# Down projection of groups 0 and 1 as seven products per pair of output halves, in a stage of its own behind the walks, with operands passed through device memory

## The chip, the cores and the metric

The kernel runs on one core of a Trainium2 chip. The metric is the device time of one execution in microseconds (us). Engines are named as the profile names them: PE is TensorE (PEld its weight loads), DVE is VectorE, ACT is ScalarE, POOL is GpSimd, SP is the engine in whose queue most DMAs are issued. L126 is line 126 of the kernel.

## The reference, cut to what matters

One decoder layer on 1024 prompt tokens and 8 x 4 decode tokens, 1056 in all, of width 1024, in float32: a mixing sub-layer (pooling and windowed attention), a dense feed-forward of width 2816, and a per-layer input gated by a sigmoid.

```
x = x + _rms(mix, n_mix_post)
f = _rms(x, n_ffn_pre)
f = (jax.nn.silu(f @ w_gate) * (f @ w_up)) @ w_down
x = x + _rms(f, n_ffn_post)
x = x + jax.nn.sigmoid(x @ w_ple_gate) * (p @ w_ple)
```

The change is about `@ w_down`: a (1056 x 2816) by (2816 x 1024) product.

## The kernel before

**Tokens and numbers.** Tokens stand in columns, in three groups of 352 (`G`, `N`); features stand in partitions, 128 at a time. Each float32 product is made of three matmuls: every operand is split into a rounded high part and the rest (`split`, L163: ACT casts, DVE subtracts), and `gemm` (L291) issues high x high, high x low, low x high. All matmuls come from `mm` (L124), so all have line L126; all splits have L164 (ACT) and L165 (DVE), and are told apart by their tiles.

**Walks.** The hidden width is 22 chunks of 128, two to a slab, 11 slabs. `WALK` visits slabs 0 to 4 for group 2 alone, slabs 5 to 10 for all three groups, then slabs 0 to 4 again for groups 0 and 1. `gate_up` (L984) makes one chunk (a slot). For group 2 it makes gate and up directly, 24 matmuls each. For groups 0 and 1 it uses seven products instead of eight (a scheme of Winograd's): the 2 x 2 blocks are (group 0, group 1) x (gate, up) x two halves of the inner dimension; products P1, P2 (on B21), P4 (on T4), S2, S3, S1, S4, 12 matmuls each, 84 in a slot. Their operands B11, B21, B22, T1 to T4 (`f7`) are made once before the walks. The weights of S1 to S4 are sums and differences of the gate and up weights, formed in place in the raw tiles by four POOL operations (`w_sums`, L958) after the raw tiles have been split as they are; then the sums are split too (`sh`, `sl`).

**Down, before.** After the first products of the next slab, `downs` (L1134) multiplies the slab's hidden tile: per group eight output chunks (m) of 6 matmuls, 48 per group and slab, each evicted from PSUM into the sum `o` (ACT copies the first slab's, DVE adds the others, L1065). So a slot that follows a finished slab holds 48 more matmuls for each group walked. The hidden values stay in SBUF (`hid_put`, L955), split into `hid`.

**Weights.** `ITEMS` lists all weight work in the order of use; `need` (L270) makes each item a few ahead (`LOOK` = 4). Raw tiles (`wr`) have three buffers (`W_RAW`), loaded by SP in order; split tiles (`wp`) have eight, that is four pairs. A slot of `gate_up` takes a raw tile for gate and one for up, and four pairs: gate, up, and two of sums.

**Order.** PE's instructions in this part are kept in program order; the other engines' queues are ordered by a scheduler when the program is built, and each engine runs its queue in that order. `turn` and `chain` (L852, L865) spread the steps of a generator (`ffn_steps`, `ple_steps`) over the matmuls issued: `share` sets how densely, and the second argument of `chain` after how many matmuls it begins.

**The end, before.** Behind the walks: one `ple_out` of group 2, the last down products of group 0 and then of group 1, 48 matmuls each; `ple_steps(0)` starts 24 matmuls after group 0's last, `ple_steps(1)` 54 after group 1's. `ple_steps` scales by the norm and the gain and adds the residual (L1104, L1108), makes the operands of a further seven-product scheme for the per-layer gate (`e_sum`, L1082: T1 to T4), while PE runs seven more `ple_out` of group 2, 30 matmuls each, then four `ple_first` (L1188), then four `ple_rest` (L1201).

## Time and profile before

| | before |
|---|---|
| time, median of 3 runs | 1134.59 us (1134.0 to 1137.2) |
| span of the profiled execution | 1132.5 us |
| PE busy | 1111.7 us, 7067 matmuls |
| PEld busy | 1087.4 us |
| DVE busy | 783.6 us |
| ACT busy | 454.3 us |
| POOL busy | 199.0 us |
| DMA | 102.16 MB, mean 90 GB/s |
| granted PE clock, mean | 0.995 |

The span runs from the first to the last instruction of one profiled execution; the times of the runs are of other executions, and their median lies 2.1 us above that span. Busy time is the time in which an engine had an instruction under way; matmuls overlap one another, so the pace of PE is read from how many start in a stretch. Idle time before an instruction is put down to what released it (`<-`).

### The profile page before, as it was taken

To read this page: it belongs to the slowest core of one execution; us is meant where nothing else is said; L and a number is where in the kernel's file an instruction comes from. 1 tells how busy PE (TensorE), PEld (TensorE's weight loads), DVE (VectorE), ACT (ScalarE), POOL (GpSimd) and SP (SyncE) were. 2 spreads that over 40 slices of the span, in tenths; PEclk is the share of its full clock that TensorE was granted. 3 is DMA by queue.
4 is the path that set the end of the run, shared out by engine and by line. 5 is a ranking of instruction groups with operands and counts; after the bars stand their busy time and mean duration, and the time that the engine had idled before them with its cause. 6 is when DMAs were issued, how large, how long until landed. Compare 5 with 4: busy or idle time off the path is not lost. (4 is left out here: it accounts for less than half of the span.)

```text
span 1132.5 us, 17606 instructions
## 1 busy us (share of the span) xinstructions
PE 1111.7 (98%) x7067; PEld 1087.4 (96%) x7067; DVE 783.6 (69%) x1283; ACT 454.3 (40%) x793; POOL 199.0 (18%) x165
## 2 busy tenths in 40 slices
PE   8999999999999999999999999999999999999797
PEld 8999987799999999999999999999999999999697
DVE  6666457876888965355554556547887877789786
ACT  7322266764555523331321313123424334364432
POOL 0044032200000042011111101111141132100231
PEclk9999999999999999999999999999999999999899
DMA  8121310172553312111110212122112222427041
GB/s 285 56 69 56 113 50 20 44 274 74 187 189 117 131 38 76 38 53 60 38 57 19 75 38 75 38 88 76 61 52 94 75 69 94 143 82 258 31 156 58
DMA packets 35985, 102.16 MB, mean 90 GB/s; under 512 B 4260, under 2 KB 14788, under 8 KB 35904
## 3 DMA queue, kind: packets, MB, share of 16 engines
q1 hardware_dynamic: 34576, 99.27, 25.8%
q10 hardware_dynamic: 1328, 1.77, 0.5%
q8 instruction: 55, 0.90, 0.3%
q14 instruction: 26, 0.21, 0.1%
HBM read 90.92 MB, written 10.11 MB: 89 GB/s over the span
## 5 line engine op out<-in xcount | busy, mean ns | idle before, releaser
L126 PE MATMUL b<-hid,wh 128*128 128x352 f32 x1056 | 252.7, 322 | 1.4 <-DVE o L1104 0.8
L164 ACT CAST wh<-wr 128x1024 fp32r<-128x1024 f32 (+1 forms) x135 | 138.4, 1029 | 249.3 <-PE b L126 205.6
L126 PE MATMUL b<-fh,wh 128*128 128x352 f32 x712 | 230.5, 324 | 0.0
L126 PE MATMUL b<-fl,wh 128*128 128x352 f32 x712 | 228.8, 321 | 0.0
L126 PE MATMUL b<-fh,wl 128*128 128x352 f32 x712 | 228.7, 321 | 0.0
L968 POOL TENSOR_TENSOR wr<-wr 128x512 f32<-128x512 f32 x52 | 74.3, 1428 | 738.7 <-DVE wl L165 451.9
L165 DVE TENSOR_TENSOR wl<-wr,wh 128x1024 fp32r<-128x1024 f32 (+1 forms) x135 | 165.4, 1229 | 40.2 <-ACT wh L164 39.9
L126 PEld LDWEIGHTS b<-hid,wh 128*128 128x128 f32 x1056 | 182.5, 188 | 2.2 <-PE b L126 1.1
L126 PE MATMUL b<-hid,wl 128*128 128x352 f32 x528 | 169.1, 320 | 0.0
L1065 DVE TENSOR_TENSOR o<-o,b 128x352 f32<-128x352 f32 x240 | 115.0, 514 | 29.5 <-PE b L126 29.4
L126 PEld LDWEIGHTS b<-fl,wh 128*128 128x128 f32 x712 | 134.4, 189 | 0.0
L126 PE MATMUL b<-fh,sh 128*128 128x352 f32 x416 | 134.3, 323 | 0.0
L126 PEld LDWEIGHTS b<-fh,wh 128*128 128x128 f32 x712 | 134.2, 188 | 0.0
L126 PEld LDWEIGHTS b<-fh,wl 128*128 128x128 f32 x712 | 134.1, 188 | 0.0
L126 PE MATMUL b<-fh,sl 128*128 128x352 f32 x416 | 133.5, 321 | 0.0
L126 PE MATMUL b<-fl,sh 128*128 128x352 f32 x416 | 133.3, 320 | 0.0
L165 DVE TENSOR_TENSOR sl<-wr,sh 128x1024 fp32r<-128x1024 f32 x52 | 63.5, 1222 | 84.5 <-ACT sh L164 84.5
L164 ACT CAST sh<-wr 128x1024 fp32r<-128x1024 f32 x52 | 53.9, 1047 | 144.4 <-POOL wr L968 104.8
L126 PE MATMUL b<-h,wh 128*128 128x352 f32 x480 | 105.8, 326 | 1.5 <-ACT h L379 1.1
L126 PEld LDWEIGHTS b<-hid,wl 128*128 128x128 f32 x528 | 98.9, 187 | 0.0
L126 PEld LDWEIGHTS b<-h,wh 128*128 128x128 f32 x480 | 82.5, 190 | 2.4 <-ACT h L379 1.3
L126 PEld LDWEIGHTS b<-fl,sh 128*128 128x128 f32 x416 | 78.3, 188 | 0.0
(175 smaller groups left out, 1695.4 us busy)
## 6 DMA issues: line engine op xcount, KB each, us to landing
wr<-in_w_gu_dram SPq DMA_DIRECT2D x64, 512.0 KB, 3.3
wr<-in_w_dn_dram SPq DMA_DIRECT2D x32, 512.0 KB, 3.3
wr<-in_w_pg_dram SPq DMA_DIRECT2D x18, 512.0 KB, 3.5
x<-in_x_dram SPq DMA_DIRECT2D x6, 704.0 KB, 10.6
x1d<-x SPq DMA_DIRECT2D x6, 704.0 KB, 3.6
x<-x1d SPq DMA_DIRECT2D x6, 704.0 KB, 5.5
out_y_dram<-yo SPq DMA_DIRECT2D x24, 176.0 KB, 1.9
wr<-in_w_out_b_dram SPq DMA_DIRECT2D x8, 512.0 KB, 4.2
```

Of the source, the lines that this page charges most:

```text
L126: ins = te.matmul(*args, **kw)
L164: fix(se.copy(hi, src))
L165: fix(ve.tensor_tensor(lo, src, hi.bitcast(F32), op=ALU.subtract))
L968: ge.tensor_tensor(out, a, b, op=op)
L1065: ve.tensor_tensor(o, o, v, op=ALU.add)
```

## The change

The down product of group 2 stays where it was. For groups 0 and 1 it leaves the walks and becomes a stage behind them, `down7`, as seven products per pair of output halves instead of eight: the 2 x 2 blocks are now (group 0, group 1) x (even, odd chunk of a slab) x (output columns 0 to 511, 512 to 1023).

- **Operands.** `gate_up` ends in `pair_put`. After a slab's first slot it stages B11 and, after a POOL subtraction, T1; after the second B21, B22 and, after three POOL subtractions, T2, T3 and T4. `stage` splits each (ACT and DVE: seven splits per slab, four before) and, when both slabs of a set are there, writes the tile to device memory (`xd`; 35 DMAs of 704 KB and 7 of half that). The slabs are grouped in the order of the walk into five sets of two and one of a single slab (slab 4). Four new buffers (`hk`) hold the values meanwhile; `tmp` has five buffers instead of six, and the pool of activation tiles 29 instead of 27.
- **Weights.** `q_load` loads the quarters of `w_down` of a set (`wq`, 512 KB). The quarters of P1, P2 and P4 are split as they are; after P4's split, `q_sum` forms the sums of S1, S3, S2, S4 in place on POOL, which are then split.
- **The stage.** `STEPS` has 19 steps: all seven products on sets 0 and 1, five (P1, P2, P4, S2, S3) on sets 2 and 3, the same five on sets 4 and 5, then S1 and S4 on sets 2 to 5. A step makes four output chunks; with two sets of two slabs that is 48 matmuls. `x_get` loads the operands (`xo`) of the current step and the next two. The first seven steps copy PSUM into seven sums `u` (ACT), the later ones add (DVE); on the last use the sums are combined (`finished` also takes the squares for the norm and applies the gain, on ACT, for all groups).
- **The end.** `ple_steps(0)` starts 24 matmuls into the last two steps (S1, S4), `ple_steps(1)` 24 after them; then come all eight `ple_out` of group 2, then `ple_first` and `ple_rest` as before. `ple_steps` no longer applies the gain: per half a multiplication by the norm and one addition.

**VectorE in the late walks.** These are DVE's rows from the multiplication that ends one chunk for groups 0 and 1 (`u`) to the first evictions of the next (`p`). `sl` and `wl` are the low parts of split weights, `hid` the low part of a hidden value, `c` and `p` evictions of products, `fl` is an operand of the per-layer gate. Before, from a slab's first chunk to its second:

```order
L165 TENSOR_TENSOR sl_8211<-wr_8029,sh_8210 128x1024
L1046 TENSOR_TENSOR u_8251<-u_8251,p_8031 128x352
L165 TENSOR_TENSOR hid_8217<-u_8251,hid_8217 128x352
L1002 TENSOR_TENSOR c_8325<-p_8310,b_8326 128x352
L165 TENSOR_TENSOR fl_8340<-x_7811,fh_8339 128x1408
L165 TENSOR_TENSOR wl_8232<-wr_8136,wh_8231 128x1024
L165 TENSOR_TENSOR wl_8305<-wr_8214,wh_8304 128x1024
L1002 TENSOR_TENSOR p_8310<-p_8310,b_8368 128x352
```

And now, from a slab's second chunk to the next slab, where `st` is a staged operand; `c_7779`, `c_7919` and `u_7764` are POOL's results for T2, T4 and T3:

```order
L168 TENSOR_TENSOR sl_7868<-wr_7731,sh_7867 128x1024
L1136 TENSOR_TENSOR u_7904<-u_7904,p_7826 128x352
L168 TENSOR_TENSOR st_7956<-u_7904,st_7956 128x352
L168 TENSOR_TENSOR st_7960<-c_7779,st_7960 128x352
L1094 TENSOR_TENSOR c_7992<-p_7977,b_7993 128x352
L168 TENSOR_TENSOR wl_7887<-wr_7824,wh_7886 128x1024
L168 TENSOR_TENSOR st_7964<-c_7919,st_7964 128x352
L168 TENSOR_TENSOR st_7968<-u_7764,st_7968 128x352
L168 TENSOR_TENSOR wl_7972<-wr_7871,wh_7971 128x1024
L1094 TENSOR_TENSOR p_7977<-p_7977,b_8041 128x352
```

Instead of one `hid` there are four staged splits, and the second `wl` (`wr_7871`, the up weights of the slot after the one that begins here) stands behind all of them.

**SP at the end of the walks.** These are SP's rows there. Before, only weights and a residual (`x1d`) are loaded:

```order
L174 DMA wr_9289<-in_w_gu_dram 128x1024
L174 DMA wr_9394<-in_w_ple_dram 128x1024
L174 DMA wr_9472<-in_w_pg_dram 128x1024
L174 DMA wr_9493<-in_w_dn_dram 128x1024
L1099 DMA x_9867<-x1d_2466 128x1408
```

Now come the last spills (`xd`) of slab 4 and then the first operands (`xo`):

```order
L1024 DMA xd_8554<-st_8551 128x704
L1024 DMA xd_8559<-st_8556 128x704
L1024 DMA xd_8565<-st_8562 128x704
L1024 DMA xd_8571<-st_8568 128x704
L1024 DMA xd_8577<-st_8574 128x704
L1185 DMA xo_8579<-xd_4842 128x1408
L1185 DMA xo_8581<-xd_5797 128x1408
L1185 DMA xo_8583<-xd_5029 128x1408
L1185 DMA xo_8585<-xd_5984 128x1408
L1185 DMA xo_8587<-xd_5043 128x1408
L1185 DMA xo_8589<-xd_5998 128x1408
```

The loads of `xo`, which read what was written long before (`xd_4842`, `xd_5797`), stand behind the writes of the last slab.

The core of the diff:

```diff
-A_SLOTS = 27
+A_SLOTS = 29
...
-        return spool.tile([P, n], dt, tag="tmp", bufs=6, name=nm(s), padded_shape=[P, NX])
+        return spool.tile([P, n], dt, tag="tmp", bufs=5, name=nm(s), padded_shape=[P, NX])
+
+    def kept(s):
+        return spool.tile([P, N], F32, tag="hk", bufs=4, name=nm(s))
...
+    ORDER = list(range(AHEAD, NSLAB)) + list(range(AHEAD))
+    SETS = [ORDER[i : i + 2] for i in range(0, NSLAB, 2)]
+    QUARTER = {"P1": "11", "P2": "12", "P4": "22"}
+    FIVE, TWO = ("P1", "P2", "P4", "S2", "S3"), ("S1", "S4")
+    OPERAND = {"P1": "B11", "P2": "B21", "P4": "T4", "S2": "T2", "S3": "T3", "S1": "T1", "S4": "B22"}
+    STEPS = [(k, (0, 1)) for k in FIVE + TWO]
+    STEPS += [(k, at) for at in ((2, 3), (4, 5)) for k in FIVE]
+    STEPS += [(k, (2, 3, 4, 5)) for k in TWO]
+    WDN = {}
+    for k, at in STEPS:
+        for e in at:
+            WDN[k, e] = item("quarter" if k in QUARTER else "dsum", k, e)
...
+    def q_load(q, e):
+        if (q, e) not in quarters:
+            n = len(SETS[e])
+            t = act_tile([P, n, 512], s="wq")
+            s0 = SETS[e][0]
+            row, col = int(q[1]) - 1, int(q[0]) - 1
+            nc.sync.dma_start(t, w_dn[s0 : s0 + n, col, :, row, :].rearrange("s p n -> p s n"))
+            quarters[q, e] = t
+        return quarters[q, e]
...
+    def q_sum(k, e):
+        out, a, b, op = {
+            "S1": ("22", "21", "22", ALU.add),
+            "S3": ("21", "11", "21", ALU.subtract),
+            "S2": ("11", "22", "11", ALU.subtract),
+            "S4": ("12", "12", "11", ALU.subtract),
+        }[k]
+        ge.tensor_tensor(q_load(out, e), q_load(a, e), q_load(b, e), op=op)
...
+            elif kind == "quarter":
+                made[i] = q_split(q_load(QUARTER[js[0]], js[1]))
+                if js[0] == "P4":
+                    for n in ("S1", "S3", "S2", "S4"):
+                        q_sum(n, js[1])
...
-    def hid_put(g, slot, ht):
-        split(new_hid[g][:, slot, :], new_hid[g][:, SLAB + slot, :], ht)
+    def hid_put(slot, ht):
+        split(new_hid[0][:, slot, :], new_hid[0][:, SLAB + slot, :], ht)
+
+    def stage(key, pair, src):
+        e = next(i for i, ps in enumerate(SETS) if pair in ps)
+        i = SETS[e].index(pair)
+        if (key, e) not in staged:
+            staged[key, e] = act_tile([P, 2, 2, N], F32R, "st")
+        t = staged[key, e]
+        split(t[:, i, 0, :], t[:, i, 1, :], src)
+        if i == len(SETS[e]) - 1:
+            d = dpool.tile([P, 2, 2, N], F32, name=nm("xd"))
+            nc.sync.dma_start(d[:, : i + 1], t[:, : i + 1].bitcast(F32))
+            spilled[key, e] = d
+
+    def pair_put(pair, slot, h0, h1):
+        def sub(out, a, b):
+            ge.tensor_tensor(out, a, b, op=ALU.subtract)
+        if slot == 0:
+            stage("B11", pair, h0)
+            sub(h0, h1, h0)
+            stage("T1", pair, h0)
+            evens[:] = h0, h1
+            return
+        t1, b12 = evens
+        stage("B21", pair, h0)
+        stage("B22", pair, h1)
+        sub(t1, h1, t1)
+        stage("T2", pair, t1)
+        sub(h0, h0, t1)
+        stage("T4", pair, h0)
+        sub(b12, h1, b12)
+        stage("T3", pair, b12)
...
-        hid_put(1, slot, u3)
+        pair_put(pair, slot, c21, u3)
...
+    def x_get(n):
+        if n < len(STEPS):
+            k, at = STEPS[n]
+            for e in at:
+                key = OPERAND[k]
+                if (key, e) not in xops:
+                    w = len(SETS[e])
+                    t = act_tile([P, 2, 2, N], F32R, "xo")
+                    nc.sync.dma_start(t[:, :w].bitcast(F32), spilled[key, e][:, :w])
+                    xops[key, e] = t
+
+    def down7(n):
+        k, at = STEPS[n]
+        final = n >= len(STEPS) - len(FIVE + TWO)
+        for i in range(n, n + 3):
+            x_get(i)
...
+        def part(j, e):
+            wh, wl = need(WDN[k, e], 2)
+            x = xops[OPERAND[k], e]
+            cols = slice(j * P, (j + 1) * P)
+            ops = [(wh[:, i, cols], wl[:, i, cols], x[:, i, 0, :], x[:, i, 1, :]) for i in range(len(SETS[e]))]
+            gemm(banks[j][:, :N], ops, e == at[0], e == at[-1])
+            turn(3 * len(ops))
...
+            if n < len(FIVE + TWO):
+                se.copy(u[k], v)
+                continue
+            add(u[k], u[k], v)
...
-    hid[:] = new_hid
-    for m in range(FIRST):
+    chain(ple_steps(0), 24)
+    down7(len(STEPS) - 2)
+    down7(len(STEPS) - 1)
+    share[0] = 0.7
+    chain(ple_steps(1), 24)
+    for m in range(KC):
         ple_out(m, 2)
-    for m in range(KC):
-        last_down(END, m, 0)
-    chain(ple_steps(0), 24)
-    for m in range(KC):
-        last_down(END, m, 1)
-    chain(ple_steps(1), 54)
-    for m in range(FIRST, KC):
-        ple_out(m, 2)
-    finish(chains[:1])
+    finish(chains[:-1])
```

More of the change, by code (lines that the diff above doesn't have):

```diff
@@ L286, in need @@
             for kind, js in ITEMS[i + 1 : i + 3]:
-                for j in js:
-                    w_load(j)
+                if kind not in ("quarter", "dsum"):
+                    for j in js:
+                        w_load(j)
+            for kind, js in ITEMS[i + 1 : i + 7]:
+                if kind in ("quarter", "dsum"):
+                    q_loads(kind, js)
         return made[k]
@@ L982, in quarter, with gate_up @@
         return tuple(t[:, 4 * h : 4 * h + 4, :] for t in w)
-    def gate_up(items, slot, gs, pending):
+    def gate_up(items, pair, slot, gs, pending):
         ig, iu, is_ = items
@@ L1019, in gate_up @@
             ve.tensor_tensor(sl, sl, direct(wu), op=ALU.mult)
-        for g in gs:
+        if 2 in gs:
             if slot == 0:
-                new_hid[g] = half(g, F32R, "hid")
-        if 2 in gs:
-            hid_put(2, slot, sl)
+                new_hid[0] = half(2, F32R, "hid")
+            hid_put(slot, sl)
         if pending and 0 not in gs:
@@ L1039, in gate_up @@
         ve.tensor_tensor(c21, c21, c11, op=ALU.mult)
-        hid_put(0, slot, c21)
         p5 = product(s["S1"], f7["T1"])
@@ L1130, in ple_steps @@
                 yield 20, 0
-    END = len(WALK) - 1
     def downs(n):
-        s, gs = WALK[n]
         hid[:] = old_hid
-        for half_m in (range(4), range(4, KC)):
-            for g in (2, 0, 1):
-                for m in half_m:
-                    if g in gs:
-                        (last_down if g == 2 and s == NSLAB - 1 else down)(n, m, g)
-        if s == NSLAB - 1:
+        for m in range(KC):
+            down(n, m)
+            if WALK[n][0] == NSLAB - 1:
+                finished(m, 2)
+        if WALK[n][0] == NSLAB - 1:
             share[0] = 0.1
@@ L1150, in trunk_kernel @@
         for i in range(SLAB):
-            gate_up(WGU[n][i], i, gs, (lambda: downs(n - 1)) if i == 0 and n else None)
+            first = i == 0 and n and 2 in WALK[n - 1][1]
+            gate_up(WGU[n][i], s, i, gs, (lambda: downs(n - 1)) if first else None)
+    share[0] = 0.3
+    for n in range(len(STEPS) - 2):
+        down7(n)
     finish(list(chains))
-    share[0] = 0.7
     def ple_end(gate, wp, m, g):
```

116 lines of the change are left out of this document (80 added, 36 removed).

## The prediction

> **What bounds it now.** I read the page's busy table, then the stretches, then who waits for whom, then the order of time in one of the late slots. The columns of a stretch are each engine's busy time, its instructions in brackets, granted clock, DMA share, GB/s.
>
> ```profile
> PE 1111.7 (98%) x7067; PEld 1087.4 (96%) x7067; DVE 783.6 (69%) x1283; ACT 454.3 (40%) x793; POOL 199.0 (18%) x165
> 500.00:600.00 100.00, 100.00 (x632) 100.00 (x631) 56.94 (x96) 24.37 (x36) 15.96 (x12) 1.00 0.16 53
> 900.00:1000.00 100.00, 100.00 (x632) 100.00 (x631) 77.03 (x125) 39.95 (x57) 22.13 (x16) 1.00 0.32 110
> PE b L126 <- ACT p L1196: 5.9, 1, 5.9
> PE b L126 <- DVE dg L325: 1.2, 2, 0.8
> SPq L174 <- DVE sl L165: 470.8, 48, 28.6
> ```
>
> TensorE is the bound: 632 matmuls in 100 us, 0.158 us each at full clock, and the longest wait of PE in the run is one of 5.9 us in the tail. So each matmul taken away is worth 0.158 us, as long as everything else still keeps ahead. The last row shows what may not: weight loads sit in SP's queue until VectorE has finished a split (`sl`) that frees one of three raw buffers. That costs PE nothing today.
>
> **Matmuls removed.** All three groups' down products read `hid`:
>
> ```profile
> L126 PE MATMUL b<-hid,wh 128*128 128x352 f32 x1056 | 252.7, 322 | 1.4 <-DVE o L1104 0.8 <-DVE hid L165 0.6
> L126 PE MATMUL b<-hid,wl 128*128 128x352 f32 x528 | 169.1, 320 | 0.0
> L1065 DVE TENSOR_TENSOR o<-o,b 128x352 f32<-128x352 f32 x240 | 115.0, 514 | 29.5 <-PE b L126 29.4
> L1108 DVE SCALAR_TENSOR_TENSOR x<-o,c,x 128x352 f32<-128x352 f32 x24 | 15.2, 661 | 0.0
> ```
>
> 1584 for three groups, 1056 for groups 0 and 1. Seven products take 7 x 11 pairs x 4 x 3 = 924. 132 fewer at 0.158: **-20.9 us**. Of VectorE's 240 adds of 0.51 us into `o`, 160 go and 76 into the seven sums come; ScalarE evicts the first round (28 copies for 16) and takes over the scaling from the 24 operations of 0.66. VectorE, at 69%, becomes freer by this, and PE does not wait for any of it at present (its wait list has only single waits of about a microsecond besides the one above): nothing.
>
> **The tail.** PE's columns around its one long wait:
>
> ```profile
> 1060.00:1065.00 5.00, 1.48 (x10) 1.19 (x8) 5.00 (x4) 0.73 (x1) 0.00 (x0) 1.00 0.00 0
> 1065.00:1070.00 5.00, 2.65 (x9) 2.65 (x10) 3.72 (x4) 2.43 (x4) 3.56 (x2) 0.58 0.00 0
> 1070.00:1075.00 5.00, 5.00 (x26) 5.00 (x25) 0.90 (x1) 1.99 (x3) 2.82 (x3) 0.74 0.00 0
> ```
>
> 45 matmuls run where 95 fit: 50 x 0.158 = 7.9 us lost, 5.9 of it idle and 2.0 at the clock that is granted after it. The wait is for ScalarE's copy of the first `ple_first` product (the row "PE b L126 <- ACT p L1196" above); in ScalarE's order that copy stands behind the cast of T4, the last step of group 1's chain. Now group 1's chain starts 24 instead of 54 matmuls after its last product and has eight `ple_out` instead of seven ahead of that copy (60 matmuls, 9.5 us, more), group 0's chain no longer competes with it, and the copy stands ahead of those casts. I take **-7**, from -8 to -3, since VectorE stays crowded there.
>
> **The late walks.** In slabs 0 to 4, walked last, a slot of `gate_up` is 84 matmuls, 13.3 us. Until now every second slot also had 96 matmuls (15.2 us) of down products; these are gone. What has to fit into a slot is the cycle of weights. One such cycle before (start, duration):
>
> ```profile
> 917.51 4.92 SPq L174 DMA_DIRECT2D wr<-in_w_gu_dram  x2
> 926.26 0.32 PE L126 MATMUL b<-fh,sh 128*128 128x352 f32 x1
> 926.34 1.05 ACT L164 CAST wh<-wr 128x1024 fp32r<-128x1024 f32 x1 [0.85 <-PE b L126]
> 927.43 1.23 DVE L165 TENSOR_TENSOR wl<-wr,wh 128x1024 fp32r<-128x1024 f32 x1 [0.68 <-ACT wh L164]
> 928.78 1.29 POOL L968 TENSOR_TENSOR wr<-wr 128x512 f32<-128x512 f32 x1 [13.64 <-DVE wl L165]
> 933.14 1.45 POOL L968 TENSOR_TENSOR wr<-wr 128x512 f32<-128x512 f32 x1
> 934.62 2.00 ACT L164 CAST sh<-wr 128x1024 fp32r<-128x1024 f32 x2 [2.20 <-POOL wr L968]
> 935.70 1.23 DVE L165 TENSOR_TENSOR sl<-wr,sh 128x1024 fp32r<-128x1024 f32 x1 [1.83 <-ACT sh L164]
> ```
>
> The up weights' load is issued when the former `sl` ends (X = 917.5). From the end of `wl` (928.7) to the end of the next `sl` (936.9) it takes 8.2 us: four GpSimd sums, a cast, a subtraction. S2 of this slot began at 926.3, 8.8 after its sums were ready; S2 of the next is 84 matmuls on, at 939.6, only 2.7 after its own. So a short slot used up 6 us of lead, and the long slot gave it back. Now no long slot follows.
>
> How early can `wl` end after X? The load lands after 3.3 and cast and subtraction take 2.3, so with 8.2 the cycle is 13.8 at least. But VectorE's order puts the operands of the pair just finished ahead of that `wl`. Before, without GpSimd in it:
>
> ```profile
> 938.41 0.52 DVE L1046 TENSOR_TENSOR u<-u,p 128x352 f32<-128x352 f32 x1
> 939.48 0.53 DVE L165 TENSOR_TENSOR hid<-u,hid 128x352 fp32r<-128x352 f32 x1 [0.55 <-ACT hid L164]
> 941.94 1.23 DVE L165 TENSOR_TENSOR wl<-wr,wh 128x1024 fp32r<-128x1024 f32 x1 [0.28 <-ACT wh L164]
> L968 POOL TENSOR_TENSOR wr<-wr 128x512 f32<-128x512 f32 x52 | 74.3, 1428 | 738.7 <-DVE wl L165 451.9
> L552 POOL TENSOR_TENSOR a<-a,a 128x16 f32<-128x16 f32 x4 | 0.9, 224 | 0.3
> wr<-in_w_gu_dram SPq DMA_DIRECT2D x64, 512.0 KB, 3.3
> ```
>
> From 936.9 to the end of that `wl`, the second of two, at 943.2 it was 6.3; the multiplication ended 2.0 after X. Now a GpSimd subtraction of 352 columns follows it; on the line through 16 columns (0.22) and 512 (1.43) that is 1.0 us. After a slab's first slot there is one (T1). By the orders of ScalarE and VectorE come then T1's cast 0.5, the gate weights' cast 1.05, a silu 0.5, the up weights' cast 1.05 and `wl` 1.2: 2.0 + 1.1 + 4.3 = 7.4. After the second slot there are three in a row (T2, T3, T4), then T4's and T3's casts, the silu, the up weights' cast and `wl`: 2.0 + 3.1 + 0.5 + 0.5 + 0.5 + 1.05 + 1.2 = 8.9. VectorE runs its rows in order, so `wl` cannot pass the staged splits, and GpSimd's sums wait for it.
>
> The cycles are thus 7.4 + 8.2 = 15.6 and 8.9 + 8.2 = 17.1 where PE's slot is 13.3: each slab loses 2.3 + 3.8. The lead to start from is at most 2.6 (P4 frees the tiles that the cast needs, the row at 926.34, and S2 of the next slot is 13.3 behind that, its sums 10.7). From slab 0's second slot to slab 4's second there are eight cycles, four of each: 24.4 - 2.6 = **+22**, as PE's waits before S2. Ends: at 13.8 it is 8 x 0.5 - 2.6, about 1, or nothing where the lead lasts; with two more handovers of a us each, 38. I take the middle, because the order of the rows fixes it. PE's other work there hides none of this: products run in the written order, and S2 is the first to need the sums.
>
> The spills themselves, 42 DMAs of 704 or 352 KB, go through SP ahead of some weight loads. The load that the cycle hangs on is in SP's order directly behind spills whose splits VectorE has done earlier, so I charge nothing; were it to land later than 6 us after X, the lateness would count. In the walks with group 2 (slabs 5 to 10) a slot is 132 or 180 matmuls, 20.9 or 28.5 us, and covers a cycle of 17.
>
> **From the walks to the products.** The first loads of `xo` stand in SP's queue behind the last spill (T3 of slab 4), and PE has nothing else. After the last product:
>
> ```profile
> L1045 ACT ACTIVATE p<-p 128x352 f32<-128x352 f32 x22 | 11.0, 498 | 20.7 <-DVE p L1002 20.7
> L1046 DVE TENSOR_TENSOR u<-u,p 128x352 f32<-128x352 f32 x22 | 11.4, 520 | 3.5 <-ACT p L1045 3.4
> L164 ACT CAST hid<-u 128x352 fp32r<-128x352 f32 x22 | 10.7, 484 | 7.8 <-DVE u L1046 7.5
> x<-in_x_dram SPq DMA_DIRECT2D x6, 704.0 KB, 10.6
> x<-x1d SPq DMA_DIRECT2D x6, 704.0 KB, 5.5
> DMA to landing us min/median/max: 3.1/5.5/12.1
> ```
>
> (the last row is of all loads into `x`).
>
> Add 0.5; a staged split and one of 1.2 us that stand before the multiplication, 1.6; multiplication 0.5; three subtractions 3.0; cast 0.5; two splits 1.0; handovers 0.3; SP's issues 0.3: 7.7. A load of the same 704 KB takes 5.5 where few are in flight, 10.6 where six follow one another, as six do here, behind spills: 8. Then 2.0 for the clock, as in the tail. **+18**, from 10 (3.1 was the shortest landing, no clock) to 23. By the Trainium skill, "DMA: Bandwidth & Descriptors", section "Queues, rings and completion order", each DMA engine consumes descriptors in ring order, so the first two of the six would land before the others. By that rule an estimate is 5 instead of 8 (two at the 370 GB/s quoted below, 3.9, and 1.1 that the shortest landing takes beyond its own share), and this term 15; the median of 10.6 over six loads issued together speaks against it.
>
> **In the new stage.** The weights' sums are now made by GpSimd per set of two pairs, in place: P4's quarter must be split before the first sum overwrites it, and S2's second half is the seventh of eight operations in GpSimd's order.
>
> ```profile
> L648 POOL TENSOR_TENSOR a<-a,sm 128x1056 f32<-128x1056 f32 x2 | 3.9, 1950 | 7.9 <-DVE sm L646 7.5 <-ACT y L764 0.4
> 235.00:240.00 5.00, 5.00 (x36) 4.85 (x35) 2.50 (x7) 3.18 (x6) 0.00 (x0) 1.00 1.06 370
> 225.00:230.00 5.00, 5.00 (x36) 4.98 (x36) 2.52 (x4) 1.74 (x4) 0.00 (x0) 1.00 0.75 233
> ```
>
> 1024 columns take 1.95 to 2 x 1.43; I take 2.2. The pair tiles come free 6.7 us into a round (P1's last use), split 2.3, seven sums 15.4, split 2.3: 26.7. PE wants the second half at 3 x 7.6 + 0.9 = 23.7: 3 lost, 1 in the first round, which starts at the low clock, 2 in the last, whose second set is half: **+6**, 0 to 16. Transfers: 27.7 MB of operands (35 tiles of 704 KB, 7 of half that) and 7.3 MB of quarters (11.5 less the eight loaded during the walks) in 924 x 0.158 = 146 us, 240 GB/s; 370 has been reached, so I charge nothing; the cover is the prefetch of two steps, 15 us. The rest of a step (two casts of 1.05, two splits of 1.2, four evictions of 0.5) lies beside its 48 matmuls, 7.6 us of PE.
>
> **Sum.** Against the profiled span of 1132.5: -20.9 - 7 + 22 + 18 + 6 = +18.1, so 1150.6. The median is 2.1 above that span: **1152.7**.
>
> **Rivals.**
> *The weights keep up* (faster). Place: PE's wait for S2 in the late slots. If `wl` gets through before the staged splits hold it up, the +22 is 0: 1152.7 - 22 = 1130.7. For: the least cycle, 13.8, is only 0.5 above PE's slot. Against: VectorE's order. It decides at half a microsecond: with more lost there the run is within 0.3% of before (about what a measurement of this kernel tells from none) or slower.
>
> *GpSimd and VectorE take turns*:
>
> ```profile
> 909.42 1.45 POOL L968 TENSOR_TENSOR wr<-wr 128x512 f32<-128x512 f32 x1 [16.66 <-DVE wl L165]
> 910.28 0.98 DVE L165 TENSOR_TENSOR hid<-u,hid 128x352 fp32r<-128x352 f32 x1 [0.55 <-ACT hid L164]
> ```
>
> Beside a GpSimd operation this split took 0.98 instead of 0.52. Two microseconds more in each of eight cycles: +16, 1169. For: the new subtractions put both engines side by side. Against: only two or three such operations lie on the path. The Trainium skill, "SBUF — State Buffer", section "SBUF: two separate sides", has it as an exclusive lock for the whole instruction against VectorE operations with two SBUF inputs; the 0.98 agrees, though the split lost 0.46 and not a whole 1.45.
>
> *Transfers bind the new stage.* Seven steps load two operands and two quarters, 2.5 MB in 7.6 us. At the 233 GB/s of the start of a burst they take 10.7: +22, 1175. For: SP issues in order, and loads wait for slots that PE frees. Against: 370 GB/s a little later.
>
> **Chances and range.** Forecast as summed (1138 to 1165) 0.58; the weights keep up, wholly or nearly, 0.22 (0.13 faster, 0.09 within 0.3%); turns 0.12; transfers 0.08. Slower in all 0.78. The range takes the first rival in nearly to its time and reaches past the third, for the unknown ends of the transition and the sums: 1129 to 1176.
>
> **What would show it.** PE's waits for `sl` or `wl` in the last five slabs, 2 to 4 us per slot, some 22 in all; one wait of about 16 us for `xo` at the first `down7`, with the clock low after it; waits for `ql` at each S2; no 5.9 us wait in the tail; 924 matmuls on `xo`. I am wrong if the late slots run at 13.3 us, or if PE's wait at the passage is under 10.

## The result, and the profile after

| | before | after |
|---|---|---|
| time, median | 1134.88 us (1134.0 to 1137.2) | 1204.64 us (1201.94 to 1207.45) |
| ratio | | 1.0613 (95% interval 1.059 to 1.0637) |
| span of the profiled execution | 1132.5 us | 1202.9 us (its time 1204.64 us) |
| PE busy, matmuls | 1111.7 us, 7067 | 1122.8 us, 6935 |
| granted PE clock, mean | 0.995 | 0.964 |

One further execution of the changed kernel took 6152.56 us and is left out of the comparison. The forecast was 1152.7 us, from 1129 to 1176: slower was right, but the loss is 70 us and not 18.

The busy table and PE's waits of the changed kernel (in all, times, longest):

```profile
PE 1122.8 (93%) x6935; PEld 1092.4 (91%) x6935; DVE 840.2 (70%) x1246; ACT 507.9 (42%) x891; POOL 319.8 (27%) x233
```

```profile
PE b L126 <- DMA xo<-xd: 22.2, 3, 16.1
PE b L126 <- DVE acc L830: 15.3, 3, 6.3
PE b L126 <- ACT sh L167: 13.5, 6, 3.9
PE b L126 <- ACT qh L167: 9.1, 2, 4.6
PE b L126 <- DVE sl L168: 4.0, 7, 1.0
PE b L126 <- DVE ql L168: 3.1, 3, 1.5
```

There are 132 matmuls fewer, yet PE has waits that add up to 67 us where before it had one of 5.9 and some of about 1. The wait of 5.9 for ScalarE's copy is gone; the other rows are new. How much each place costs, the low clock included, is read from the stretches: the length less the matmuls begun times the full pace of 0.158 us. After:

```profile
690.00:730.00 40.00, 33.11 (x195) 32.54 (x194) 34.10 (x50) 24.22 (x42) 15.98 (x12) 0.91 0.46 166
745.00:872.00 127.00, 110.46 (x625) 106.83 (x624) 99.75 (x134) 55.42 (x85) 57.22 (x44) 0.92 0.49 175
872.00:899.00 27.00, 10.95 (x53) 10.61 (x52) 7.96 (x14) 6.26 (x12) 3.26 (x3) 0.68 0.86 323
899.00:1045.00 146.00, 127.62 (x730) 125.34 (x729) 79.17 (x93) 46.42 (x71) 58.88 (x24) 0.91 0.57 201
1045.00:1100.00 55.00, 45.82 (x258) 44.97 (x258) 39.82 (x63) 27.26 (x41) 0.00 (x0) 0.88 0.34 120
1100.00:1150.00 50.00, 49.08 (x305) 48.50 (x304) 44.43 (x49) 23.59 (x33) 8.11 (x5) 1.00 0.41 129
1150.00:1202.90 52.90, 45.62 (x281) 44.41 (x279) 38.44 (x62) 14.46 (x22) 15.39 (x11) 0.98 0.29 98
```

Before, in the four stretches of its last 350 us that lose anything:

```profile
790.00:890.00 100.00, 98.58 (x617) 97.86 (x616) 82.44 (x125) 35.18 (x46) 25.23 (x19) 1.00 0.19 64
990.00:1055.00 65.00, 63.10 (x397) 61.77 (x397) 60.02 (x99) 37.39 (x53) 0.00 (x0) 1.00 0.47 159
1055.00:1080.00 25.00, 19.07 (x103) 18.49 (x102) 19.56 (x20) 9.73 (x14) 7.87 (x6) 0.86 0.17 49
1080.00:1132.50 52.50, 46.40 (x288) 45.83 (x286) 39.49 (x64) 15.06 (x23) 15.01 (x11) 0.98 0.29 98
```

For the late walks (745 to 872), for instance, that is 127 - 625 x 0.158 = 28.3; of it 127 - 110.46 = 16.5 is idle, the rest, 11.7, low clock. The whole account:

| place | forecast | measured, worked out from the rows |
|---|---|---|
| 132 matmuls | -20.9 | -20.9 |
| tail | -7 | 1.8 + 8.5 after, 8.7 + 7.0 before: -5.4 |
| late walks | +22 | 28.3, less 2.5 that before lost there (790 to 890): +25.8 |
| passage to the products | +18 | 18.6 |
| new stage | +6 | 146 - 730 x 0.158 = 30.7 |
| group 2's norm (690 to 730) | 0 | 9.2 |
| norms of groups 0 and 1 (1045 to 1100) | 0 | 55 - 258 x 0.158 = 14.2, less 2.3 that before lost there (990 to 1055): +11.9 |
| sum | +18 | +69.9, and the spans differ by 70.4 |

Four of the terms have about the size that was forecast. The stage is 25 us dearer, and three waits for `acc` (23 us with the clock behind them) were not in the sum at all. What is behind the terms, the runs have to show; each is timed against the kernel before on the same chip, and its ratio is to that.

### The profile page after: what moved, and what is told of

It reads as the page before. It is cut to its first block, busy times and chain, and to the rows that moved or that the text cites. A ratio compares the mean times of both kernels' runs of the same rounds, so it can differ in the third digit from the quotient of the medians.

```text
span 1202.9 us, 17720 instructions
## 1 busy us (share of the span) xinstructions
PE 1122.8 (93%) x6935; PEld 1092.4 (91%) x6935; DVE 840.2 (70%) x1246; ACT 507.9 (42%) x891; POOL 319.8 (27%) x233
## 5 line engine op out<-in xcount | busy, mean ns | idle before, releaser
L167 ACT CAST wh<-wr 128x1024 fp32r<-128x1024 f32 (+1 forms) x125 | 128.0, 1027 | 167.8 <-PE b L126 129.4
L126 PE MATMUL b<-xo,qh 128*128 128x352 f32 x616 | 159.1, 343 | 31.4 <-DMA xo<-xd 22.2
L168 DVE TENSOR_TENSOR wl<-wr,wh 128x1024 fp32r<-128x1024 f32 (+1 forms) x125 | 154.9, 1243 | 41.3 <-ACT wh L167 33.0
L126 PEld LDWEIGHTS b<-xo,qh 128*128 128x128 f32 x616 | 116.3, 205 | 32.8 <-issue 20.9
L126 PE MATMUL b<-fh,sl 128*128 128x352 f32 x416 | 138.5, 333 | 4.0 <-DVE sl L168 4.0
L168 DVE TENSOR_TENSOR ql<-wq,qh 128x1024 fp32r<-128x1024 f32 (+1 forms) x42 | 55.3, 1336 | 78.0 <-ACT qh L167 66.9
L126 PE MATMUL b<-xo,ql 128*128 128x352 f32 x308 | 104.7, 340 | 3.2 <-DVE ql L168 3.1
L167 ACT CAST sh<-wr 128x1024 fp32r<-128x1024 f32 x52 | 53.4, 1045 | 120.9 <-POOL wr L1060 120.9
L126 PEld LDWEIGHTS b<-fh,sh 128*128 128x128 f32 x416 | 81.4, 196 | 15.2 <-ACT sh L167 15.2
L126 PEld LDWEIGHTS b<-fh,sl 128*128 128x128 f32 x416 | 81.3, 195 | 6.5 <-DVE sl L168 6.4
L126 PE MATMUL b<-hid,wh 128*128 128x352 f32 x352 | 84.4, 322 | 0.6 <-DVE c L1094 0.6
## 6 DMA issues: line engine op xcount, KB each, us to landing
x<-in_x_dram SPq DMA_DIRECT2D x6, 704.0 KB, 10.9
```

Of the source, the lines that this page charges most:

```text
L126: ins = te.matmul(*args, **kw)
L167: fix(se.copy(hi, src))
L168: fix(ve.tensor_tensor(lo, src, hi.bitcast(F32), op=ALU.subtract))
```

## Experiments on the late walks

The forecast had two bounds for a turn of the weights' cycle: one over three raw buffers and, longer, one over the rows of ScalarE and VectorE, with staged operands ahead of `wl`. One turn after the change; the rows are of ScalarE, GpSimd, VectorE and PE, in order of time:

```profile
842.14 1.04 ACT L167 CAST sh<-wr 128x1024 fp32r<-128x1024 f32 x1 [8.24 <-POOL wr L1060]
...
846.90 0.50 ACT L1135 ACTIVATE p<-p 128x352 f32<-128x352 f32 x1 [2.04 <-DVE p L1094]
...
848.95 1.93 POOL L1032 TENSOR_TENSOR u<-u,u 128x352 f32<-128x352 f32 x1
...
850.00 1.26 DVE L168 TENSOR_TENSOR st<-u,st 128x352 fp32r<-128x352 f32 x1
...
852.10 0.49 ACT L167 CAST st<-c 128x352 fp32r<-128x352 f32 x1 [2.58 <-POOL c L1032]
...
852.88 1.05 ACT L167 CAST wh<-wr 128x1024 fp32r<-128x1024 f32 x1
853.96 1.23 DVE L168 TENSOR_TENSOR wl<-wr,wh 128x1024 fp32r<-128x1024 f32 x1 [0.38 <-ACT wh L167]
...
855.27 1.29 POOL L1060 TENSOR_TENSOR wr<-wr 128x512 f32<-128x512 f32 x1 [3.20 <-DVE wl L168]
...
860.82 1.99 ACT L167 CAST sh<-wr 128x1024 fp32r<-128x1024 f32 x2 [6.49 <-POOL wr L1060]
...
861.91 0.66 PE L126 MATMUL b<-fh,sh 128*128 128x352 f32 x1 [3.94 <-ACT sh L167]
```

ScalarE casts the sums, then runs the silu that ends the former pair; GpSimd's subtractions and the staged splits follow. ScalarE's cast `wh`, which `wl` needs, stands behind the cast of T4, which waits 2.58 for a subtraction. Then come `wl`, GpSimd's sums, and ScalarE's next cast, for which PE waits 3.94. From one `sh` to the next it takes 18.7 us here, and PE's slot is 13.3. The S2 waits at 760.10 and 861.91, six slots apart, give 17.0 per slot.

**A fourth raw buffer (raw4).**

```diff
-W_RAW = 3
+W_RAW = 4
-A_SLOTS = 29
+A_SLOTS = 28
```

> Four raw weight buffers for three, one activation slot fewer (28), all else as in the changed kernel (1204.6). If the late slots hang on the cycle last sl -> load -> wl -> sums -> sl, the load now comes a whole slot earlier: PE's waits for sh and sl between 745 and 872 us (16.5 of idle, 28.1 lost with the low clock) fall under 6, and the time falls by 20 to 28, to 1177 to 1185. If GpSimd and VectorE themselves are the limit (sums 6.8, subtractions, splits stretched beside GpSimd), the slots stay at 16 to 17 us and the time falls by less than 8. The passage to the products, the stage and the three norm waits stay as they are under both.

1205.66 us (ratio 1.0627, 1.0609 to 1.0645): nothing. From 745 to 872 there are 642 matmuls, a loss of 25.6; S2 waits at 762.00 and 861.28 give 16.5 per slot. The last of the walks' weights had been issued by 831 instead of 844, and `wl` ended 10.0 us behind the slot's first `sl`, in the changed kernel 10.7. So the raw buffers are not what holds the slots, which agrees with the forecast: its least cycle over the buffers, 13.8, was below its cycles over the rows. (The edit also takes one activation slot away; what that costs by itself no run shows.)

**Extra matmuls ahead of S2 (walk_warm).**

```diff
+        if 2 not in gs:
+            idle = bank()
+            for _ in range(20):
+                mm(idle[:, :n], f7["B22"][0][:, 0, :P], f7["B22"][0][:, 0, :], start=True, stop=True)
         add(p1, p1, product(s["S2"], f7["T2"]))
```

> 20 extra matmuls of 3.2 us ahead of S2 in each of the ten late slots (200 in all, 31.6 us of PE; their result is not used). If the weights' cycle of about 18 us sets the late slots, PE has 3 to 4 us to spare in each and the extra work is free: time within 8 us of 1204.6, waits for sh/sl down from 16.5 to under 6, no low clock left there. If the 11.6 us of low clock behind those waits stand on the path on top of the cycle, the time falls by 6 to 12. If PE is what sets the slots, the time rises by 20 to 32.

1203.41 us (1.0612, 1.0597 to 1.0628): 200 matmuls, 31.6 us of PE, at no cost in time. From 745 to 872 PE is never idle and never slow:

```profile
745.00:872.00 127.00, 126.92 (x798) 126.63 (x796) 99.28 (x133) 53.89 (x83) 57.57 (x44) 1.00 0.51 183
```

798 - 625 = 173 more matmuls stand in the same 127 us. PE is a passenger there, and the low clock behind its waits (11.7 us in the changed kernel) lies inside the weights' cycle: it costs nothing of its own.

**Splits of the pair behind the next weights' splits, order held (defer_fix).**

```diff
-        pair_put(pair, slot, c21, u3)
+        late.append((pair, slot, c21, u3))
...
         wg = need(ig)
+        if late:
+            pair_put(*late.pop())
...
+        fixed[0] = 2 not in gs
```

> A finished pair's subtractions and splits are written behind the next slot's weight splits, and in the late slots the splits are held to the written order on ScalarE and VectorE, so that wl no longer stands behind staged splits (one activation slot fewer, 28, to hold two more results). With a fourth raw buffer the late slots lost as much as before (25.4 us), so the buffer is not what closes the cycle. If the rows do (sh casts, silu, multiplication, subtractions, staged splits, then wh and wl, then the sums), the slots come down to 13.3 to 14.5, PE's waits for sh and sl from 16.5 to under 5, and the time falls by 18 to 26, to 1179 to 1187. If GpSimd and VectorE standing in each other's way set the pace, whatever the order, the time falls by under 8. If the held order makes ScalarE wait for tiles, it rises.

1209.97 us (1.0674, 1.0655 to 1.0693): a little worse. S2 waits at 767.27 and 865.40 give 16.4 per slot. One turn of it:

```profile
824.15 1.23 DVE L168 TENSOR_TENSOR wl<-wr,wh 128x1024 fp32r<-128x1024 f32 x1 [0.88 <-ACT wh L167]
825.50 1.45 POOL L1060 TENSOR_TENSOR wr<-wr 128x512 f32<-128x512 f32 x1 [2.49 <-DVE wl L168]
826.92 1.22 POOL L1032 TENSOR_TENSOR c<-c,c 128x352 f32<-128x352 f32 x1
828.11 3.10 POOL L1060 TENSOR_TENSOR wr<-wr,wr 128x512 f32<-128x512 f32 x2
```

In the last three turns `wl` now ended 6.0 to 6.6 us behind the first `sl` (in the changed kernel 8.4 to 10.7), but a subtraction now stood among GpSimd's sums, as here, and from `wl` to the next `sl` it took 9.2 to 10.9 (there 7.9 to 9.3). The order moved the work to another part of the cycle and did not take it out; group 2's norm wait grew to 11.1. (Here too there is one activation slot fewer, and two more `hk` buffers.)

**What GpSimd and VectorE each do (subs_dve, sums_dve, st_pool).** The pair's subtractions to VectorE; the weight sums of the short slots to VectorE; the low parts of the staged operands to GpSimd:

```diff
         def sub(out, a, b):
-            ge.tensor_tensor(out, a, b, op=ALU.subtract)
+            ve.tensor_tensor(out, a, b, op=ALU.subtract)
```

> The four subtractions of a finished pair on VectorE instead of GpSimd. They are in the weights' cycle: 1.0 us after a first slot, 3 to 4.1 after a second, and the splits beside them take 1.26 to 1.6 instead of 0.52. If that is what lengthens the cycle over the slot, on VectorE they cost 0.5 each and nothing stretches: cycle shorter by 0.5 and 3 us, late walks lose 28 - 8 x 1.7 = 14 instead of 28, time 1190. If the rest of the cycle (load 3.3, sums 6.8, casts) is what matters, the time falls by under 5.

```diff
-            ge.tensor_tensor(out, a, b, op=op)
+            sums_on[0].tensor_tensor(out, a, b, op=op)
...
+        sums_on[0] = ge if 2 in gs else ve
```

> In the late slots the four weight sums of a slot on VectorE (about 0.7 each for 512 columns) instead of GpSimd (1.4 each, 5.5 to 6.8 in a row). VectorE is busy 99.8 of the 127 us from 745 to 872, 13.3 per slot. If the slow stretch of sums in the cycle is what the slots wait for, the cycle gets 3 shorter and the slots come to 14 to 14.5: time falls by 15 to 22. If VectorE's own load in its row is the limit (13.3 + 2.7 - some 1.5 that it lost beside GpSimd = 14.5, with the waits that it has anyway), the slots stay at 16 to 17: time within 6 of 1204.6.

```diff
-        split(t[:, i, 0, :], t[:, i, 1, :], src)
+        se.copy(t[:, i, 0, :], src)
+        ge.tensor_tensor(t[:, i, 1, :], src, t[:, i, 0, :].bitcast(F32), op=ALU.subtract)
```

> The low parts of the staged operands (seven per pair of slots) are made by GpSimd (about 1.0 each) instead of VectorE. If VectorE's load is the limit of the late slots (13.3 us of it per slot, 3 of them staged splits), its row gets 3 us shorter per slot: time falls by 12 to 22. If GpSimd's part of the cycle is the limit, 3.5 us more per slot on it make it longer: time rises by 5 to 25.

subs_dve 1198.01 us (1.0558, 1.0542 to 1.0575), 6.6 less; sums_dve 1195.50 (1.0536, 1.0519 to 1.0554), 9.1 less; st_pool 1217.72 (1.074, 1.0715 to 1.0764), 13.1 more. These edits also act on the walks with group 2, so the late walks are read alone, from group 2's norm matmuls (714.91 in the changed kernel) to the last product: 157.2 us in the changed kernel, 151.2 in subs_dve, 143.3 in sums_dve, 161.4 in st_pool. Work taken from GpSimd shortens the cycle. Of the 13.9 that sums_dve gains there, 3.4 are lost ahead of the norm and 2.7 at the passage; of st_pool's loss, 4.2 are in the late walks and 9.4 ahead of them. With the sums on VectorE the S2 waits at 791.01 and 851.52, four slots apart, give 15.1, and VectorE is then busy almost throughout:

```profile
742.00:860.00 118.00, 108.60 (x656) 105.50 (x655) 110.45 (x162) 55.99 (x85) 19.32 (x15) 0.99 0.54 192
```

**No staging in the last five slabs (no_stage).**

```diff
+        if pair in ORDER[6:]:
+            for key in OPERAND.values():
+                for e in (3, 4, 5):
+                    spilled[key, e] = spilled[key, e - 3]
+            return
```

> Work left out: in the five last slabs the finished pairs are not subtracted, split and spilled; the products read the operands of the first three sets in their place. If the staging is what stretches the cycle (2 to 4 of GpSimd per pair, 3 of VectorE per slot), the late slots fall to 13.3 to 14.3, the walks' loss from 28 to under 8, and the passage has no spills to wait for (18.6 to 8 to 12): time 1172 to 1182. If sums, casts and splits of the weights alone exceed a short slot, the slots stay above 15, and only the passage gains: 1190 to 1198.

The products then read the operands of the first three sets. 1162.82 us (1.025, 1.0231 to 1.0268): 41.8 less, more than either expectation. The late slots run at PE's pace, and at the passage PE waits for no `xo` any more:

```profile
745.00:872.00 127.00, 123.88 (x765) 121.56 (x764) 87.65 (x114) 49.33 (x67) 53.55 (x34) 1.00 0.47 170
```

127 - 765 x 0.158 = 6.1 lost where it was 28.3. From the end of one slot's first `sl` to the next slot's it takes 13.7 to 14.2 in the last six turns, in the changed kernel 15.2 to 18.7. So weights, sums and splits alone nearly fit into a short slot; the staging of a pair (subtractions, splits, writes) is what closes the cycle, and with the passage it is 42 of the 70 us. Which of its parts does it, no single edit shows: they stand in three rows that wait for one another.

**The slabs in another order (mixed).**

```diff
-    WALK += [(s, (0, 1, 2)) for s in range(AHEAD, NSLAB)]
-    WALK += [(s, (0, 1)) for s in range(AHEAD)]
+    ORDER = [5, 6, 0, 1, 7, 8, 2, 3, 9, 10, 4]
+    WALK += [(s, (0, 1) if s < AHEAD else (0, 1, 2)) for s in ORDER]
```

> The same slabs in another order: two with group 2, two without, and so on (5, 6, 0, 1, 7, 8, 2, 3, 9, 10, 4), so that at most four short slots follow one another and eight long ones no longer stand alone. If a short slot loses only when the lead from the long slots is gone (some 6 to 9 us of it), each run of four loses 4 x 3.6 - 7 at most: the loss in the walks (28 and the 9 of group 2's norm ahead of them) falls to 12 to 22: time 1183 to 1194. If each short slot loses its 3.6 whatever stands before it, the time stays within 5 of 1204.6.

1197.52 us (1.055, 1.0532 to 1.0568): 7.1 less, between the two expectations. Each run of four short slots has its longest wait in its last (2.0 at 554.3, 2.4 at 718.0), so the long slots do build a lead, but one that lasts for fewer than four.

## Experiments on the passage, the stage and the norms

**The last spills from ScalarE (spill_act).**

```diff
-            nc.sync.dma_start(d[:, : i + 1], t[:, : i + 1].bitcast(F32))
+            q = nc.scalar if pair == ORDER[-1] and key not in ("B11", "T1") else nc.sync
+            q.dma_start(d[:, : i + 1], t[:, : i + 1].bitcast(F32))
```

> The last five spills (second slot of slab 4) are issued by ScalarE, so that the first loads of xo no longer stand behind them in SP's queue. If the order in SP is what holds the first xo (issued at 882.5, landed at 888.4, PE waits 16.05), the loads start as soon as their slots are free, at 866 to 876, and PE's wait at the first product falls to 0 to 8: time 1190 to 1199. If the slots only come free after the last pair's products, or the loads then share the rates with the spills, the wait stays at 12 to 16 and the time within 4 of 1204.6.

1195.90 us (1.0541, 1.0522 to 1.0559): 8.7 less. SP's queue in the changed kernel:

```profile
875.60 6.78 SPq L1024 DMA_DIRECT2D xd<-st  x5
882.47 15.87 SPq L1185 DMA_DIRECT2D xo<-xd  x12
```

and here, with PE's first product:

```profile
870.71 0.50 SPq L177 DMA_DIRECT2D wr<-in_w_pg_dram  x1
871.33 18.02 SPq L1186 DMA_DIRECT2D xo<-xd  x8
```

```profile
877.96 0.92 PE L126 MATMUL b<-xo,qh 128*128 128x352 f32 x2 [5.99 <-ACT st L167]
```

The loads start 11 us earlier, and PE waits 6.0 instead of 16.05. The order in SP's queue held them, as forecast.

**Two output blocks of group 2 in the passage (fill_pass).**

```diff
+    for n in range(3):
+        x_get(n)
+    for m in range(EARLY):
+        ple_out(m, 2)
     share[0] = 0.3
```

> Two of group 2's eight output blocks (60 matmuls, 9.5 us) are computed in the passage between the walks and the products instead of in the tail, and the loads of xo are issued ahead of them. If the passage is only a hole in PE's work, they fill it and its loss falls from 18.6 to about 9; in the tail they no longer cover group 1's chain, which VectorE finishes some 4 us ahead of its use: 5 come back there, time falls by 3 to 6, to 1199 to 1202. If the tail has more slack than that, the whole 9.5 is won: 1195. If the extra weights delay the last slots, no gain.

1201.64 us (1.0602, 1.0587 to 1.0618): 3.0 less. They fill most of the hole (PE still waits 5.6 at the first product), and the tail gets two waits, of 7.6 and 4.4, for group 1's operands. The tail has no cover to lend.

**The stage's sums on VectorE (qsum_dve).**

```diff
-        ge.tensor_tensor(q_load(out, e), q_load(a, e), q_load(b, e), op=op)
+        ve.tensor_tensor(q_load(out, e), q_load(a, e), q_load(b, e), op=op)
```

> The 24 sums of quarters in the stage on VectorE (1.1 to 1.2 each) instead of GpSimd (about 2.2). If the chain P4 split, seven sums, S2 split is what PE waits for (4.6 + 1.5, twice, with half clock behind them), the waits for qh and ql (12.2 of idle) go and the low clock behind them, about 6 to 8: time falls by 12 to 20, to 1185 to 1193. If the splits wait for tiles of pairs or for the quarters' loads, it falls by under 4.

1180.82 us (1.041, 1.0394 to 1.0425): 23.8 less, above the expectation. The sums in the changed kernel by group, and here:

```profile
L312 POOL TENSOR_TENSOR wq<-wq,wq 128x1024 f32<-128x1024 f32 x20 | 52.9, 2664 | 87.4 <-DVE ql L168 87.1
```

```profile
L312 DVE TENSOR_TENSOR wq<-wq,wq 128x1024 f32<-128x1024 f32 x20 | 23.4, 1218 | 0.0
```

2.66 us a sum where the forecast took 2.2. Seven of them come to 18.6 instead of 15.4, so the second half's operand comes 3 + 3.2 = 6.2 late, and PE waited 4.6 + 1.5 = 6.1 in each of the first two rounds. These 12.2 and the low clock behind them are gone here, and one of the waits for `xo` (4.4) with them.

**Later norms (late_norms).**

```diff
-            chain(ple_steps(2), 19)
+            chain(ple_steps(2), 80)
...
-    chain(ple_steps(0), 24)
+    chain(ple_steps(0), 64)
...
-    chain(ple_steps(1), 24)
+    chain(ple_steps(1), 64)
```

> The chains of the three last norms start later: group 2's 80 matmuls behind its last product instead of 19, those of groups 0 and 1 64 instead of 24. If PE waits there only because acc is still being added up when the chain's first matmuls come (6.3, 3.6, 5.5 of idle and 7.3 of low clock around them), these three waits go: time falls by 15 to 23, to 1182 to 1190. If what follows in the chains is then late, a wait for the operands of group 1 comes back in the tail and the time falls by under 8.

1199.97 us (1.0581, 1.0565 to 1.0597): 4.7 less; the three waits for `acc` are gone and others stand in their place:

```profile
PE b L126 <- DMA xo<-xd: 24.2, 3, 18.0
PE b L126 <- ACT sh L167: 16.6, 6, 3.6
PE b L126 <- ACT qh L167: 9.1, 2, 4.6
PE b L126 <- ACT fh L167: 5.8, 1, 5.8
PE b L126 <- DVE fl L168: 4.9, 1, 4.9
```

Group 2's came back in the walks (`sh` 3.1 more) and the passage (1.9 more): where VectorE and GpSimd set the pace, PE's own wait is free. Group 0's stayed away: from the first product on `xo` to the last it takes 179.1 us (891.60 to 1070.70) instead of 187.5 (888.46 to 1075.98). Group 1's, 5.5, came back as 10.7 us for its operands in the tail: the chain from the last product over the norm to these operands ends last there.

## The edits together

**Four, then the three that gained (four, three).** Four: spill_act, defer_fix, qsum_dve and late_norms. Three: spill_act, qsum_dve and subs_dve.

> Together: the last spills from ScalarE, pairs deferred with the order held, the stage's sums on VectorE, the norms later. If the four losses are separate places that add up: 9 + 22 + 16 + 18 = 65, so 1140. If one wait takes another's place: 1150 to 1170. What stays in either case is the loads of xo in the stage's last steps (1.8 + 4.4) and the rest of the passage.

> The three edits that gained alone, together: last spills from ScalarE (1195.9), the stage's sums on VectorE (1180.8), a pair's subtractions on VectorE (1198.0). If they are separate places, 1204.6 - 8.7 - 23.8 - 6.6 = 1165.5, within 4. If one wait takes another's place, 1170 or more.

Four came to 1168.45 us (1.0303, 1.0286 to 1.032), since two of its edits gain nothing or little; three to 1165.24 (1.0281, 1.0266 to 1.0297) where 1204.6 - 8.7 - 23.8 - 6.6 = 1165.5 was worked out: separate places.

**With the mixed walk (best_mixed, best_mixed_s).** Spill_act, qsum_dve and mixed; then sums_dve as well.

> mixed with the last spills from ScalarE and the stage's sums on VectorE. If they add: what mixed gives, less 8.7 and 23.8: 1151 to 1162 where the lead counts, 1172 where it does not.

> best_mixed with the weight sums of the short slots on VectorE. If GpSimd's slow sums are in the cycle still, another 4 to 9 less; if VectorE's load in the short slots is now the limit, within 3 of best_mixed, or more.

1159.66 us (1.0225, 1.021 to 1.0241) and 1146.72 (1.0102, 1.0075 to 1.013). The lead of the long slots now lasts for a run of four: in the two runs PE's longest waits for split sums are 0.68 and 0.51, where mixed had 2.0 and 2.4.

**And later norms (best_late, best_late1).**

```diff
-            chain(ple_steps(2), 19)
+            chain(ple_steps(2), 72)
...
-    chain(ple_steps(0), 24)
+    chain(ple_steps(0), 54)
```

> best_mixed_s with the chains of group 2 and group 0 later (72 and 54 matmuls instead of 19 and 24). Group 2's wait is 7.2 of idle and about 2 of low clock; VectorE no longer sets the walks' pace, so it should go whole: 9. Group 0's is 4.0 and 2: its later norm has eight output blocks until it is needed, and all behind it, group 1's chain too, starts earlier: 6. Time 1146.7 - 15 = 1132, from 1127 to 1138. If the waits are only exchanged for others as in late_norms: 1141 or more.

> best_late with group 1's chain later too (54 matmuls instead of 24). If PE's wait there (5.5 and 2 of low clock) is only missing cover, 6 to 8 less than best_late. If the chain from the last product over the norm to group 1's operands is what ends last, the wait comes back in the tail, and the time is within 3 of best_late.

1138.94 us (1.0036, 1.0023 to 1.0049) and 1139.68 (1.0051, 1.0035 to 1.0066): 7.8 less, half of what was expected, and no difference between the two. The waits and SP's queue of best_late:

```profile
PE b L126 <- DMA xo<-xd: 17.1, 3, 13.3
PE b L126 <- DVE acc L829: 4.5, 2, 2.8
```

```profile
840.80 0.86 SPq L1270 DMA_DIRECT2D x<-x1d  x2
841.70 4.08 SPq L1286 DMA_DIRECT2D pr<-in_p_dram  x2
845.94 13.06 SPq L1186 DMA_DIRECT2D xo<-xd  x8
```

Group 2's later chain puts its own loads (`x1d`, `p`) into SP's queue ahead of the first `xo`, and the passage waits 13.3 us again. Up to the last product of the walks (840.05, 5317 matmuls) PE has lost nothing by then, so without that wait an estimate is 1138.9 - 13.3 = 1126, below the kernel before; no run tried it. No version ran faster than the kernel before; the closest is 0.4% slower.

## Why the prediction was wrong, by its own steps

The forecast fell short by 52 us: by 25 in the new stage, by 21 at the three norms, which it had put at nothing, and by 6 in the other terms together.

- **Matmuls removed, -20.9:** right. In undisturbed stretches the pace is 0.158, and 616 + 308 = 924 matmuls read `xo`.
- **The tail, -7:** the wait for ScalarE's copy went, and the stretch behind 1100 lost 5.4 less. But the step "group 1's chain starts 24 instead of 54 matmuls after its last product" was booked as a gain without asking when `acc` is ready. PE now waits there:

```profile
1085.61 1.33 PE L126 MATMUL b<-c,acc 128*88 128x1 f32 x8 [5.47 <-DVE acc L830]
```

With group 0's (3.6) and the clock that is 14.2 us, 11.9 more than before, so the end as a whole lost 6.5. late_norms and best_late1 show that group 1's part is the chain itself: a later start moves it and does not remove it.
- **VectorE becomes freer, nothing:** this step failed too. VectorE's busy time rose from 783.6 to 840.2 us, since the staged splits came, and PE waits for it at group 2's norm (9.2). PE's matmul there before and after:

```profile
798.43 0.71 PE L126 MATMUL b<-c,acc 128*88 128x1 f32 x8
```

```profile
714.91 1.34 PE L126 MATMUL b<-c,acc 128*88 128x1 f32 x8 [6.32 <-DVE acc L830]
```

Before, group 2's last products were mixed with those of groups 0 and 1, 96 matmuls or 15.2 us, in which VectorE could add up squares. Now 48 follow one another, 7.6 us, with eight evictions and seven additions to `acc` of 0.5 each, and the weights' splits between them. The evictions also begin late, at 703.42 for products that start at 696.07, since one `wl` and four staged splits, stretched beside GpSimd, fill VectorE's row from 695.28 to 703.07. So the removed matmuls were cover for another step, and the staging made that step later; no run separates the two. In the changed kernel this wait costs little of its own, since it came back in the walks (late_norms).
- **Late walks, +22:** 25.8 measured, at the place named, S2's sums, and by the mechanism of the sum, the rows. In the last six turns the way from the end of a slot's first `sl` to the end of `wl` took 6.0, 7.3 and 8.4 after a slab's first slot (7.4 forecast) and 9.4, 8.9 and 10.7 after its second (8.9 forecast); from there to the next `sl` it took 7.9 to 9.3 (8.2 forecast). The raw buffers are not in it (raw4), the staged operands are (no_stage), but another place for `wl` in VectorE's order does not take them out (defer_fix). Of the loss only 16.5 are waits, where some 22 were to be seen; the low clock behind them fills the rest of the same turns, and that none was charged on top was right here (walk_warm).
- **The passage, +18:** 18.6: 16.05 of wait, the rest low clock; its cause, the order in SP's queue, was right (spill_act). That the number fits so well is in part luck: the first `xo` left SP's queue at 882.47, 10.4 us behind the last product of the walks (7.7 forecast), and PE began 6.0 later (8 in the sum, 5 by the prediction's other estimate).
- **The new stage, +6:** the step that failed most, by 25. A GpSimd sum was priced at 2.2, between 1.95 for 1056 columns of another addition and 2 x 1.43; it took 2.66. With seven in a row on the path, two waits of 6.1 came of that, where 1 and 3 were forecast. The clock behind short waits was charged at nothing: 146 - 127.62 = 18.4 of the stage's loss is idle, 12.3 low clock. And of "transfers: nothing", two waits for `xo` (1.8 and 4.4) came true.
- **The rivals:** "GpSimd and VectorE take turns" was priced at 16 in the late walks. subs_dve puts the subtractions' whole part, on the path and in stretched splits, at 6.6: some of it is there, beside the forecast term, not in its place. The split at 850.00 took 1.26 instead of 0.52, 0.74 longer, and the subtraction beside it ended 0.88 after the split began (848.95 + 1.93). The Trainium skill, "SBUF — State Buffer", section "SBUF: two separate sides", speaks of an exclusive lock, and 0.74 of 0.88 roughly agrees. "The weights keep up" is refuted. "Transfers bind" holds only for 6.2 us of waits.

## What to carry to other kernels

Ask of each piece of work that is taken from the bottleneck engine what else it covered: here 132 matmuls less saved 21 us, and the down products' leaving the walks uncovered the weights' cycle there and group 2's norm. Price operations that come to stand in a row on the path by rows of the same operation, and charge the low clock behind every wait that no other cycle hides. Test a supposed cycle with one more buffer and with the suspected work left out: the first gained nothing, the second gave 42 us.

## What the runs showed of the hardware

**A wait of 1.81 us lowered the clock.** PE waited 1.81 us once, at 1016.15 in the changed kernel, with full pace before it:

```profile
1010.00:1014.00 4.00, 4.00 (x27) 4.00 (x26) 3.93 (x4) 1.09 (x2) 4.00 (x3) 1.00 0.35 133
1014.00:1018.00 4.00, 2.19 (x12) 1.93 (x11) 3.87 (x4) 1.08 (x2) 4.00 (x3) 0.87 0.71 265
1018.00:1022.00 4.00, 4.00 (x20) 4.00 (x19) 3.24 (x4) 1.45 (x2) 4.00 (x3) 0.70 0.00 0
```

By the matmuls' starts a slow pace lasted from 1016.70 to 1020.49, 3.8 us, in which 14 began where 24 fit: 1.6 us lost, nearly as long as the wait. A wait of 1.21 us (at 761.61 in sums_dve) left the clock at 1.00. The Trainium skill, "TensorE: Matmul & The Clock Gate", section "Part 1: The HAM clock gate", lets the clock fall after an idle window of about 3.4 us and rise after as long a busy one: the 3.8 us agree with the second, the 1.81 us do not with the first.

**GpSimd against VectorE.** The same addition of 1024 columns took 2.66 us on GpSimd and 1.22 on VectorE, by the means of 20 each (the two rows at qsum_dve).
